# Gate b of the second half by block products, and weight sums taken one step behind their loads, in a hybrid RG-LRU/GLA decoder layer on one core

## The chip, the cores and the metric

The kernel runs on one core of a Trainium2 chip. The metric is the device time of one execution in microseconds. A profiled execution lists every instruction of the engines: PE (TensorE), PEld (its weight loads), DVE (VectorE), ACT (ScalarE), POOL (GpSimd) and SP (SyncE, which here only issues transfers).

## The reference

One decoder layer, for 1024 prompt tokens and 8 x 4 sample tokens that share the weights. All in float32, with a model width of 1024:

```python
h = rmsnorm(x, norm1_g) * (1 + sc1) + sh1
u_x, u_g, u_q, u_k, u_v, u_r, u_lr, u_ga, u_gb = split(h @ w_in)
y_a = rg_lru(causal_conv(u_x)) * gelu(u_g)          # first branch, recurrent, 1280 wide
y_b = norm(gated_linear_attention(u_q, u_k, u_v, u_lr)) * silu(u_r)   # second branch
m = sigmoid(u_ga) * (y_a @ proj_a) + sigmoid(u_gb) * (y_b @ proj_b)
x = x + gt1 * (m @ w_out)
f1, f2 = split(h2 @ ffn_w1)        # h2: x normed and modulated again, 2 x 2816 wide
x = x + gt2 * ((silu(f1) * f2) @ ffn_w2)
```

The change concerns the line with `m`: gate a (`u_ga`) with the product of the first, recurrent branch, and gate b (`u_gb`) with the product of the second.

## The kernel before, in words

Tokens lie along the free dimension. Half A has the first 512 of them, half B the other 512 and the 32 sample tokens (544, handled as two column parts of 272). Half A runs through all stages, then half B. A weight tile is 128 columns of the output: 8 chunks of 128 inputs each, 512 KB. Each is loaded as float32 into a tile of tag "raw" (five buffers, by SP), and split into a high and a low part ("hl", three buffers): the high part by ACT (L154), the low one by DVE (L155). A product then takes three passes a chunk: high by high, high by low, low by high (L452, L453, L454; L1434 to L1436 in the block products). The split has a raised priority (`AHEAD`), so that the scheduler pulls it ahead of other work on ACT and DVE.

*Products by blocks.* Some products are done for pairs of weight tiles by a Strassen-Winograd scheme: `products` makes 7 products of 4 chunks (12 matmuls each, 84 in all) where the plain way needs 8 (96). It needs sums of the inputs (`block_sums`: d0, d1, ta, tb, t12, t3, t4), and sums of weight blocks. These are made on the chip: a job loads two raw tiles, DVE makes four additions, and POOL stores the results to DRAM (`wsum` for FFN 1, `wsumg` for gates, `wsum2` for FFN 2), from where they are loaded as weights later. `weight_sums` (L348) makes them for whole tiles ("s1", "s2", four additions of 128x512, L352 to L355): 16 jobs, loads by SP in the "raw" buffers, sums right behind the load. `paced_sums` (L362) does half tiles of 256 or 384 columns in buffers of their own (tag "sums", two): a copy on POOL (L387) of one element of a tile just made, `pace[0]`, holds a job's loads (L388) until there; then the sums (L392 to L396) and the stores (L398); each job is taken in two steps, load and sum.

*The stages.* `branches` of a half runs the recurrent and attention branches; then `merge_b`: for each of eight tiles j the gate b (`gbps`, tanh), and the second branch's product (`pbps`, weights `proj_b`), both multiplied into `mb`, with the recurrent chain (`lru`: ug, ux, g tiles) filled in between. Then half A does `merge_a`: for each j gate a (`gaps`), the product of the recurrent branch (`paps`, two weight tiles pa0 and pa1 of 5 chunks), `join` (L1264, L1265: multiply by the gate, add to mb), `keep_m` (split of the sum). Half B does `merge_a_fast`: the first four recurrent products are held in SBUF (`pa`), and gate a is done by blocks (`gates_fast`, four blocks: `ha`, `hb`, `hc` in PSUM, `gc`, `gd` in SBUF), with the other four recurrent products behind the last blocks. Then `back`: `out_proj` (wops), norm, FFN.

Who does what when: PE's order in the block products is as written (`as_written`); elsewhere a scheduler orders each engine's work by priority and by modelled times, and buffers are taken as they come free. Each engine and each transfer queue then works strictly in its order. `behind(last)` pins an instruction behind work that was traced before it.

## Time and profile before

| what | value |
|---|---|
| three runs | 1957.03, 1960.13, 1961.34 us; median 1960.13 |
| profiled execution | 1958.39 us; its span 1956.6 us, mean granted clock 0.997 |
| busy in the span | PE 98%, PEld 90%, DVE 70%, ACT 50%, POOL 7% |
| half A's gate stage (`merge_a`) | 452.4 to 559.3 us |
| half B's `merge_b` with the recurrent chain | 1272 to 1424 us |
| half B's four held products, then gate a by blocks | 1424 to 1454, 1454 to 1527.5 us |
| full sum jobs on DVE | 16, from 272.2 to 771.7 us |

A row of the timeline reads: start in us, duration, engine, line, operation, output<-inputs, shapes; in brackets the idle time of the engine just before it and what ended it. Matmuls are pipelined, so the durations of neighbours overlap, and the distance between two starts is the pace.

### The profile page before, as it was taken

What the parts mean: (1) busy time and instruction counts of PE and PEld (TensorE: products, weight loads), DVE (VectorE), ACT (ScalarE), POOL (GpSimd) and SP (SyncE); (2) the same over time, 40 slices, a digit from 0 to 9 for tenths busy, and PEclk for the clock granted to TensorE, in tenths of its full rate; (3) what the DMA queues carried; (4) which work ended last, traced back from release to release, by engine and by line L of the source; (5) the groups of instructions that cost most, each with busy time, mean ns of one, the idle gap of its engine ahead of it and who ended that gap; (6) DMA issues with size and microseconds to landing.
All of it is one profiled execution on the core that took longest, in us unless ns stands there. A gap on an engine that the chain in (4) does not pass through costs nothing. (4 is left out here: it accounts for less than half of the span.)

```text
span 1956.6 us, 33960 instructions
## 1 busy us (share of the span) xinstructions
PE 1923.5 (98%) x13380; PEld 1754.8 (90%) x13380; DVE 1360.1 (70%) x2420; ACT 972.6 (50%) x1559; POOL 144.6 (7%) x279
## 2 busy tenths in 40 slices
PE   8999999998999999999999999999999999999997
PEld 5877777787899998998899998999999999999997
DVE  5648587765658774677664497786467688888867
ACT  4536376552235552555353366675245354656653
POOL 0000002111200000000000101031201000000000
PEclk9999999999999999999999999999999999999999
DMA  8344326567864467554331413334447534555553
GB/s 342 116 154 172 117 90 245 176 211 240 292 201 157 129 184 243 193 183 149 119 123 65 146 50 101 124 114 153 140 143 226 198 130 133 176 171 179 177 163 104
DMA packets 122240, 319.24 MB, mean 163 GB/s; under 512 B 14560, under 2 KB 29664, under 8 KB 122080
## 3 DMA queue, kind: packets, MB, share of 16 engines
q1 hardware_dynamic: 107536, 263.89, 41.6%
q0 software_dynamic: 14000, 52.62, 7.5%
q8 instruction: 105, 1.72, 0.4%
q10 hardware_dynamic: 544, 0.56, 0.1%
q14 instruction: 55, 0.45, 0.1%
HBM read 278.42 MB, written 38.59 MB: 162 GB/s over the span
## 5 line engine op out<-in xcount | busy, mean ns | idle before, releaser
L155 DVE TENSOR_TENSOR fwa_hl<-fwa,fwa_hl 128x1024 fp32r<-128x1024 f32 (+1 forms) x57 | 68.8, 1207 | 44.6 <-ACT fwa_hl L154 41.2
L155 DVE TENSOR_TENSOR fwb_hl<-fwb,fwb_hl 128x1024 fp32r<-128x1024 f32 (+1 forms) x64 | 77.2, 1207 | 27.7 <-ACT fwb_hl L154 27.4
L154 ACT ACTIVATE fwa_hl<-fwa 128x1024 fp32r<-128x1024 f32 (+1 forms) x57 | 59.3, 1040 | 44.0 <-PE fapsa L1436 10.8
L154 ACT ACTIVATE fwb_hl<-fwb 128x1024 fp32r<-128x1024 f32 (+1 forms) x64 | 66.6, 1041 | 23.4 <-PE fcpsb L1436 9.0
L452 PE MATMUL f3psa<-faa,f3a_hl 128*128 128x512 f32 x176 | 68.6, 390 | 0.6 <-ACT f3a_hl L154 0.6
L454 PE MATMUL f3psa<-faa,f3a_hl 128*128 128x512 f32 x176 | 68.5, 390 | 0.4 <-DVE f3a_hl L155 0.4
L453 PE MATMUL f3psa<-faa,f3a_hl 128*128 128x512 f32 x176 | 68.6, 390 | 0.0
L154 ACT ACTIVATE f3a_hl<-f3a_raw 128x768 fp32r<-128x768 f32 (+1 forms) x32 | 25.3, 792 | 55.7 <-PE f3psa L454 47.3
L155 DVE TENSOR_TENSOR f3a_hl<-f3a_raw,f3a_hl 128x768 fp32r<-128x768 f32 (+1 forms) x32 | 28.3, 888 | 17.0 <-ACT f3a_hl L154 16.7
L452 PEld LDWEIGHTS f3psa<-faa,f3a_hl 128*128 128x128 f32 x176 | 33.0, 188 | 7.8 <-ACT f3a_hl L154 1.0
L454 PEld LDWEIGHTS f3psa<-faa,f3a_hl 128*128 128x128 f32 x176 | 33.0, 188 | 7.6 <-DVE f3a_hl L155 0.9
L453 PEld LDWEIGHTS f3psa<-faa,f3a_hl 128*128 128x128 f32 x176 | 33.0, 188 | 6.8
L352 DVE TENSOR_TENSOR s_raw<-s_raw 128x512 f32<-128x512 f32 x16 | 11.1, 691 | 40.2 <-DMA s_raw<-in_ffn 40.2
L454 PE MATMUL wopsb<-mb,wob_hl 128*128 128x272 f32 x128 | 36.9, 288 | 0.0
L452 PE MATMUL wopsb<-mb,wob_hl 128*128 128x272 f32 x128 | 36.9, 289 | 0.0
L453 PE MATMUL wopsb<-mb,wob_hl 128*128 128x272 f32 x128 | 36.8, 288 | 0.0
L453 PE MATMUL wopsa<-ma,woa_hl 128*128 128x256 f32 x128 | 36.4, 284 | 0.0
L454 PE MATMUL wopsa<-ma,woa_hl 128*128 128x256 f32 x128 | 36.2, 283 | 0.0
L452 PE MATMUL wopsa<-ma,woa_hl 128*128 128x256 f32 x128 | 36.1, 283 | 0.0
L1621 POOL DMA_DIRECT2D out_yb<-yb x4 | 2.9, 720 | 407.5 <-DVE yb L1618 406.8
L452 PE MATMUL uxpsa<-h1a,uxpsa_hl 128*128 128x512 f32 x80 | 32.3, 403 | 0.0
L155 DVE TENSOR_TENSOR fvb_hl<-fvb,fvb_hl 128x768 fp32r<-128x768 f32 x28 | 26.8, 956 | 7.7 <-ACT fvb_hl L154 7.4
(2404 smaller groups left out, 7975.3 us busy)
## 6 DMA issues: line engine op xcount, KB each, us to landing
ada<-in_ada_w SPq DMA_DIRECT2D x48, 512.0 KB, 5.5
fwb<-wsum SPq DMA_DIRECT2D x72, 256.0 KB, 3.6
s_raw<-in_ffn SPq DMA_DIRECT2D x32, 512.0 KB, 4.1
wsum<-s_raw POOLq DMA_DIRECT2D x32, 512.0 KB, 3.9
fwa<-wsum SPq DMA_DIRECT2D x64, 256.0 KB, 3.3
fwb<-in_ffn SPq DMA_DIRECT2D x54, 256.0 KB, 3.6
fwa<-in_ffn SPq DMA_DIRECT2D x48, 256.0 KB, 3.2
woa_raw<-in_w_out SPq DMA_DIRECT2D x13, 512.0 KB, 3.5
```

Source lines behind the costliest of these rows:

```text
L154: act.activation(hl[:, 0, :n], raw[:, :n], AF.Copy)
L155: dve.tensor_sub(hl[:, 1, :n], raw[:, :n], hl[:, 0, :n].bitcast(F32))
L352: dve.tensor_add(r2[:, 512:1024], r2[:, 0:512], r2[:, 512:1024])
L452: pe.matmul(out, wh, x[:, o:o + w], start=st, stop=False)
L453: pe.matmul(out, wh, x[:, N + o:N + o + w], start=False, stop=False)
L454: pe.matmul(out, wl, x[:, o:o + w], start=False, stop=en)
L1621: (queues[j // 2 % len(queues)]).dma_start(out[:, j:j + 2, o:o + w], y2)
```

## The change

- Half B's `merge_b` is replaced by `branch_b`, which makes only the second branch's products and copies them to mb by ACT. Then the four held recurrent products, then `merge_fast`: gate b by four blocks (`k`), multiplied into mb, then gate a by four blocks (`h`) as before. Half B's recurrent chain is moved ahead by three steps before `branch_b`.
- Weight sums for gate b are needed too: 28 half jobs instead of 20. Five (before: four) begin in half A's `merge_b`, seven (four) in its `merge_a`, four (none) beside half A's `ffn1_fast`, eight (eight) in `branch_b`, four (four) in the gate b blocks.
- All jobs go through `Jobs`: a step makes the sums of the job before, then begins the next one's loads. The loads of a full job are issued by POOL instead of SP. Half A's `merge_a` begins full jobs at j = 0 to 4 instead of 0, 1, 3, 4, 6.
- The input rows of gate b's weights are put into the same order as gate a's (`KORD`).
- The first step of `block_sums` is made ahead of the first held product.

```diff
@@ -345,17 +345,39 @@
 
         return t[:, :HP].rearrange("p (m u n) -> p m u n", u=2, n=P)[:, :, u, :]
 
-    def weight_sums():
-
-        for f in range(FAST[0], NF):
-            r1, r2 = load_raw(I["ffn1"][2 * f], 1024, f"s1{f}"), load_raw(I["ffn1"][2 * f + 1], 1024, f"s2{f}")
-            dve.tensor_add(r2[:, 512:1024], r2[:, 0:512], r2[:, 512:1024])
-            dve.tensor_sub(r2[:, 0:512], r1[:, 0:512], r2[:, 0:512])
-            dve.tensor_sub(r1[:, 0:512], r2[:, 512:1024], r1[:, 0:512])
-            dve.tensor_sub(r1[:, 512:1024], r1[:, 512:1024], r1[:, 0:512])
-            pool.dma_start(wsum[f][:, 0:1024], r1)
-            pool.dma_start(wsum[f][:, 1024:2048], r2)
-            yield 1
+    class Jobs:
+
+        def __init__(s, jobs):
+            s.jobs, s.sums = iter(jobs), None
+
+        def finish(s):
+            if s.sums:
+                s.sums()
+            s.sums = None
+
+        def step(s):
+            s.finish()
+            job = next(s.jobs, None)
+            if job:
+                s.sums = job()
+
+    def full_sums(f):
+        def begin():
+            r1, r2 = [wp.tile([P, 1024], F32, tag="raw", name=f"s{k}{f}_raw", bufs=5) for k in "12"]
+            for r, t in (r1, 2 * f), (r2, 2 * f + 1):
+                pool.dma_start(r, I["ffn1"][t])
+
+            def sums():
+                last = len(traced())
+                dve.tensor_add(r2[:, 512:1024], r2[:, 0:512], r2[:, 512:1024])
+                behind(last)
+                dve.tensor_sub(r2[:, 0:512], r1[:, 0:512], r2[:, 0:512])
+                dve.tensor_sub(r1[:, 0:512], r2[:, 512:1024], r1[:, 0:512])
+                dve.tensor_sub(r1[:, 512:1024], r1[:, 512:1024], r1[:, 0:512])
+                pool.dma_start(wsum[f][:, 0:1024], r1)
+                pool.dma_start(wsum[f][:, 1024:2048], r2)
+            return sums
+        return begin
 
     pace = [None]
 
@@ -377,28 +399,35 @@
         for f in range(FAST[1], FAST[0]):
             columns(wsum[f], [I["ffn1"][2 * f + v] for v in range(2)])
         rows(0)
-        for c in range(GATES):
-            columns(wsumg[c], [I["w_in"][T_GA + 2 * c + v] for v in range(2)])
+        for t in (T_GB, T_GA):
+            for c in range(GATES):
+                columns(wsumg[t, c], [I["w_in"][t + 2 * c + v] for v in range(2)])
         rows(1)
-        for k, (u, src, to) in enumerate(jobs):
+        return [half_sums(k, *job) for k, job in enumerate(jobs)]
+
+    def half_sums(k, u, src, to):
+        def begin():
             r = [wp.tile([P, 768], F32, tag="sums", name=f"sums{k}{v}", bufs=2) for v in range(2)]
             rv = [t[:, :2 * u].rearrange("p (n u) -> p n u", n=2) for t in r]
             for v in range(2):
-                pool.tensor_copy(r[v][:, 0:1], pace[0][:, 0:1])
+                if pace[0] is not None:
+                    pool.tensor_copy(r[v][:, 0:1], pace[0][:, 0:1])
                 pool.dma_start(rv[v], src[v])
-            yield 1
-            r1, r2 = rv
-            last = len(traced())
-            dve.tensor_add(r2[:, 1], r2[:, 0], r2[:, 1])
-            behind(last)
-            dve.tensor_sub(r2[:, 0], r1[:, 0], r2[:, 0])
-            dve.tensor_sub(r1[:, 0], r2[:, 1], r1[:, 0])
-            dve.tensor_sub(r1[:, 1], r1[:, 1], r1[:, 0])
-            for v in range(2):
-                pool.dma_start(to[v], rv[v])
-            yield 1
-
-    sums_of, sums_late = weight_sums(), paced_sums()
+
+            def sums():
+                r1, r2 = rv
+                last = len(traced())
+                dve.tensor_add(r2[:, 1], r2[:, 0], r2[:, 1])
+                behind(last)
+                dve.tensor_sub(r2[:, 0], r1[:, 0], r2[:, 0])
+                dve.tensor_sub(r1[:, 0], r2[:, 1], r1[:, 0])
+                dve.tensor_sub(r1[:, 1], r1[:, 1], r1[:, 0])
+                for v in range(2):
+                    pool.dma_start(to[v], rv[v])
+            return sums
+        return begin
+
+    sums_of, sums_late = Jobs([full_sums(f) for f in range(FAST[0], NF)]), Jobs(paced_sums())
 
     class Half:
         def __init__(s, hf):
...
@@ -1191,17 +1220,15 @@
                 for t, p in s.over(tg, ps):
                     act.activation(t, p, AF.Tanh, scale=0.5)
 
-            lag = 1 - s.hf
-            if lag:
-                first(0)
+            first(0)
             for j in range(KD):
                 n = f"{s.n}{j}"
-                if j + lag < KD:
-                    first(j + lag)
-                if s.hf or 3 <= j < 7:
+                if j + 1 < KD:
+                    first(j + 1)
+                if j >= 3:
                     pace[0] = tgs[j]
-                    next(sums_late, None)
-                if j + lag < KD:
+                    sums_late.step()
+                if j + 1 < KD:
                     yield 5.2
                 tg = tgs.pop(j)
                 p2 = s.wide("pbps" + n)
@@ -1210,10 +1237,23 @@
                 for (t, p), (o, _) in zip(s.over(tg, p2), s.over(m, p2)):
                     dve.scalar_tensor_tensor(o, t, 1.0, p, op0=OP.add, op1=OP.mult)
                 s.mb.append(m)
-                if s.hf or 3 <= j < 7:
-                    next(sums_late, None)
-                if s.hf == 0 and j < 7:
-                    next(sums_of, None)
+                sums_of.step() if j < 7 else sums_of.finish()
+                yield 5.2
+
+        def branch_b(s):
+
+            s.mb = []
+            pace[0] = None
+            for j in range(KD):
+                n = f"{s.n}{j}"
+                sums_late.step()
+                ps = s.wide("pbps" + n)
+                s.gemm(ps, load_w(I["proj_b"][j], 1024, "pb" + n), 8, s.y_b)
+                m = xp.tile([P, 544], F32, tag="X", name="mb" + n)
+                for o, p in s.over(m, ps):
+                    act.activation(o, p, AF.Copy)
+                s.mb.append(m)
+                pace[0] = m
                 yield 5.2
 
         def gate_a(s, j):
...
@@ -1274,37 +1314,40 @@
             s.m = []
             for j in range(KD):
                 tg = s.gate_a(j)
-                if 1 <= j < 5:
-                    next(sums_late, None)
+                sums_late.step() if j < 7 else sums_late.finish()
                 s.join(j, tg, s.over(tg, s.branch_a(j)))
                 s.keep_m(j)
-                if 1 <= j < 5:
-                    next(sums_late, None)
-                if j % 3 < 2 and j < 7:
-                    next(sums_of, None)
-
-        def merge_a_fast(s):
+                if j < 6:
+                    sums_of.step() if j < 5 else sums_of.finish()
+
+        def merge_fast(s):
 
             s.m = []
             N, b, held = s.N, s.block_sums(s.h, "h"), []
...
+                next(b, None)
                 t = two[:, j * N:(j + 1) * N] if j < 2 else T(f"pa{s.n}{j}")[:, :N]
                 for o, p in s.over(t, s.branch_a(j)):
                     act.activation(o, p, AF.Copy)
                 held.append(t)
-                next(b, None)
             drain(b)
             units = []
-            for c in range(GATES):
-                w1, w2, sm = I["w_in"][T_GA + 2 * c], I["w_in"][T_GA + 2 * c + 1], wsumg[c]
-                units += [w1[:, 0:512], sm[:, 1536:2048], sm[:, 0:512], sm[:, 512:1024], sm[:, 1024:1536], w1[:, 512:1024],
-                          w2[:, 512:1024]]
+            for g in (T_GB, T_GA):
+                for c in range(GATES):
+                    w1, w2, sm = I["w_in"][g + 2 * c], I["w_in"][g + 2 * c + 1], wsumg[g, c]
+                    units += [w1[:, 0:512], sm[:, 1536:2048], sm[:, 0:512], sm[:, 512:1024], sm[:, 1024:1536], w1[:, 512:1024],
+                              w2[:, 512:1024]]
             begin = len(traced())
             product = s.products(units, 512, s.bs, "gw" + s.n)
             for c in range(GATES):
-                tgs = s.gates_fast(c, product)
-                next(sums_late, None)
+                tgs = s.gates_fast("k", c, product)
+                sums_late.step()
+                for m, t in zip(s.mb[2 * c:], tgs):
+                    dve.scalar_tensor_tensor(m[:, :N], t[:, :N], 1.0, m[:, :N], op0=OP.add, op1=OP.mult)
+            sums_late.finish()
+            for c in range(GATES):
+                tgs = s.gates_fast("h", c, product)
                 if c == GATES - 1:
                     s.keep_m(*range(2 * c))
                 for i in range(2):
@@ -1312,9 +1355,6 @@
                     s.join(j, tg, [(tg[:, :N], held[j])] if j < 4 else s.over(tg, s.branch_a(j)))
                     if c == GATES - 1:
                         s.keep_m(j)
-                    if j >= 4:
-                        next(sums_late, None)
-            drain(sums_late)
...
@@ -1557,6 +1597,9 @@
                     s.late = tg
                 else:
                     s.keep(f, tg)
+                if s.hf == 0 and f in (13, 15, 17, 19):
+                    pace[0] = tg
+                    sums_late.step()
                 yield 4.5
             as_written(begin, (mybir.EngineType.PE,))
 
@@ -1643,7 +1686,8 @@
                 drain(s.ffn1_fast(range(FAST[0], 11)))
                 for j, _ in enumerate(s.ffn2(0, 11, s.whole)):
                     if j % 2 == 0:
-                        next(sums_of, None)
+                        sums_of.step()
+                sums_of.finish()
                 return
...
@@ -1672,7 +1716,10 @@
-            for w in s.merge_b():
+            if s.hf:
+                for _ in range(3):
+                    next(l, None)
+            for w in s.branch_b() if s.hf else s.merge_b():
                 next(l, None)
                 next(l, None)
                 s.ada(1)
...
```

What stands where on the engines' queues now, at three places. First, DVE in half A's `merge_a` around the split of gate tile 3 (gapsa3_hl; papsa2 is the recurrent product of tile 2, which PE does just before gate tile 3; s1.. and s2.. are a full job's raw tiles, sums.. a half job's). Before:

```order
L352 TENSOR_TENSOR s215_raw_4111<-s215_raw_4111 128x512
L396 TENSOR_TENSOR sums40_3861<-sums40_3861 128x384
L353 TENSOR_TENSOR s215_raw_4111<-s115_raw_4109,s215_raw_4111 128x512
L155 TENSOR_TENSOR gapsa3_hl_4022<-gapsa3_raw_4020,gapsa3_hl_4022 128x1024
L354 TENSOR_TENSOR s115_raw_4109<-s215_raw_4111,s115_raw_4109 128x512
L355 TENSOR_TENSOR s115_raw_4109<-s115_raw_4109 128x512
L155 TENSOR_TENSOR pa0a3_hl_4060<-pa0a3_raw_4058,pa0a3_hl_4060 128x640
L1264 SCALAR_TENSOR_TENSOR gaa2_3959<-gaa2_3959,papsa2_3967 128x512
```

Now:

```order
L424 TENSOR_TENSOR sums60_3883<-sums60_3883 128x384
L1304 SCALAR_TENSOR_TENSOR gaa2_3975<-gaa2_3975,papsa2_3989 128x512
L1305 TENSOR_TENSOR mba2_2934<-gaa2_3975,mba2_2934 128x512
L155 TENSOR_TENSOR gapsa3_hl_4048<-gapsa3_raw_4046,gapsa3_hl_4048 128x1024
L189 TENSOR_TENSOR ma2_4032<-mba2_2934,ma2_4032 128x512
L372 TENSOR_TENSOR s214_raw_3942<-s214_raw_3942 128x512
L420 TENSOR_TENSOR sums71_3984<-sums71_3984 128x384
L374 TENSOR_TENSOR s214_raw_3942<-s114_raw_3941,s214_raw_3942 128x512
L422 TENSOR_TENSOR sums71_3984<-sums70_3983,sums71_3984 128x384
```

The split of gate tile 3 stood ahead of the join of tile 2 (L1264), and stands right behind it (L1304, L1305) now; the same holds for gate tiles 4 and 5. The full job's sums stand behind the split now, and are those of an earlier load.

Second, DVE in half B's gate blocks where a half job's sums stand among the splits of the weights (gwb.., one for 24 matmuls). Before, in the second of the four blocks (gcb1, gdb1):

```order
L1246 TENSOR_TENSOR gdb1_14525<-gdb1_14525 128x272
L392 TENSOR_TENSOR sums161_14512<-sums161_14512 128x384
L394 TENSOR_TENSOR sums161_14512<-sums160_14511,sums161_14512 128x384
L155 TENSOR_TENSOR gwb16_hl_14688<-gwb16_14685,gwb16_hl_14688 128x1024
L1245 TENSOR_TENSOR gcb1_14524<-gcb1_14524,hcpsb1_14523 128x272
L395 TENSOR_TENSOR sums160_14511<-sums161_14512,sums160_14511 128x384
L396 TENSOR_TENSOR sums160_14511<-sums160_14511 128x384
```

Now, at the end of the fourth gate b block (kcb3, kdb3) with job 26:

```order
L1286 TENSOR_TENSOR kdb3_14425<-kdb3_14425 128x272
L420 TENSOR_TENSOR sums261_14414<-sums261_14414 128x384
L422 TENSOR_TENSOR sums261_14414<-sums260_14413,sums261_14414 128x384
L155 TENSOR_TENSOR gwb30_hl_14598<-gwb30_14595,gwb30_hl_14598 128x1024
L1285 TENSOR_TENSOR kcb3_14424<-kcb3_14424,kcpsb3_14423 128x272
L423 TENSOR_TENSOR sums260_14413<-sums261_14414,sums260_14413 128x384
L1347 SCALAR_TENSOR_TENSOR mbb7_13640<-kdb3_14425,mbb7_13640 128x544
L424 TENSOR_TENSOR sums260_14413<-sums260_14413 128x384
L155 TENSOR_TENSOR gwb32_hl_14629<-gwb32_14626,gwb32_hl_14629 128x1024
```

The pattern within a block is the same: two sums, a split, the other two. It stands in five blocks one after the other now (jobs 23 to 27, the last in the first gate a block); before, only job 16 stood among the four blocks like this, and jobs 17 to 19 between the last recurrent products.

Third, POOL in half A's `merge_a`. Before, it issued the stores of a full job there, and SP its loads; now, around the stores of job 13:

```order
L414 COPY sums61_3884<-gaa1_3875 128x1
L415 DMA sums61_3884<-in_ffn2 128x768
L368 DMA s115_raw_4041<-in_ffn1 128x1024
L378 DMA wsum13_87<-s213_raw_3842 128x1024
L426 DMA wsumf20_108<-sums61_3884 128x768
L377 DMA wsum13_87<-s113_raw_3841 128x1024
L426 DMA wsumf20_108<-sums60_3883 128x768
L414 COPY sums70_3983<-gaa2_3975 128x1
L368 DMA s215_raw_4042<-in_ffn1 128x1024
```

POOL now issues the full jobs' loads (L368) too; those of job 15 stand before and behind the stores of job 13 (L378, L377).

## The prediction

> **What bounds the kernel now.** I read the page's head first, then the view of waits for PE (who ended its idle time, total, times, longest), then windows of the stages that the change touches, then single rows of PE, DVE, ACT and POOL there.

> ```profile
> span 1956.6 us, 33960 instructions
> PE 1923.5 (98%) x13380; PEld 1754.8 (90%) x13380; DVE 1360.1 (70%) x2420; ACT 972.6 (50%) x1559; POOL 144.6 (7%) x279
> ```

> ```profile
> engine line waited for: us in total, times, longest us
> PE gapsa L454 <- DVE gapsa_hl L155: 5.6, 2, 4.9
> PE hbpsb L1434 <- ACT t12hb L1408: 0.9, 1, 0.9
> PE hbpsb L1435 <- DVE t12hb L1409: 0.4, 1, 0.4
> ```

> ```profile
> core 0: us, PE busy (x), PEclk, DMA share, GB/s
> 452.00:466.00 14.00, 13.28 (x59) 1.00 0.78 269
> 466.00:471.00 5.00, 0.23 (x2) 0.91 0.11 44
> 471.00:477.00 6.00, 5.90 (x14) 0.51 0.89 309
> ...
> core 0: us, PE busy (x) PEld busy (x) DVE busy (x) ACT busy (x) POOL busy (x), PEclk, DMA share, GB/s
> ...
> 1272.00:1424.00 152.00, 152.00 (x1196) 150.57 (x1195) 101.61 (x184) 74.18 (x124) 41.49 (x71) 1.00 0.43 137
> ...
> 1454.00:1527.50 73.50, 72.27 (x577) 71.84 (x576) 51.17 (x78) 36.35 (x62) 9.52 (x22) 1.00 0.67 216
> ```

> PE is the bound: 1923.5 of 1956.6 us. So the time falls by what matmuls are taken away, and changes by what PE stands idle. In half B's stages (from 1272 us) PE is full. The one large hole is in half A's last gate stage, 466 to 471 us, and behind it PE runs at a granted clock of 0.51 for some 6 us.

> **The change part by part. 1, fewer matmuls.** Half B's eight tiles of gate b cost 48 matmuls each (8 chunks, 3 passes, 2 column parts): 384. By blocks they are 4 blocks of 7 products of 12: 336. Taken away: 48. The price of one is not its duration but its distance to the next:

> ```profile
> 1376.23 0.29 PE L452 MATMUL gbpsb4l<-h1b,gbpsb_hl 128*128 128x272 f32 x1
> 1382.21 0.29 PE L452 MATMUL pbpsb4l<-ybb,pbb_hl 128*128 128x272 f32 x1
> 1388.18 0.29 PE L452 MATMUL gbpsb5l<-h1b,gbpsb_hl 128*128 128x272 f32 x1
> ```

> A tile of 48 starts 5.98 and 5.97 us after the one before, so 0.1245 us a matmul. The blocks run at the same pace; the first snapshot of block 0 and that of block 1 on ACT:

> ```profile
> 1457.40 0.38 ACT L1442 ACTIVATE gcb<-hapsb 128x272 f32<-128x272 f32 x1
> 1467.86 0.40 ACT L1442 ACTIVATE gcb<-hapsb 128x272 f32<-128x272 f32 x1 [1.03 <-PE hapsb L1436]
> ```

> That is 10.46 us for 84, again 0.1245. Saving: 48 x 0.1245 = **-6.0 us**. The operand sums t12, on which PE waited 0.9 + 0.4 us, now begin a step earlier, beside the four held recurrent products (first DVE rows of block_sums ahead of the first of those): **-1.3**.

> **2, half A's gate stage.** The hole's origin stands on DVE: the sums of a full job (L352 to L355) wait for their load, and the split of the next gate tile (L155) stands behind them in DVE's order.

> ```profile
> 465.85 0.39 PE L453 MATMUL gapsa<-h1a,gapsa_hl 128*128 128x512 f32 x1
> 471.10 0.79 PE L454 MATMUL gapsa<-h1a,gapsa_hl 128*128 128x512 f32 x1 [4.86 <-DVE gapsa_hl L155]
> 473.40 0.63 PE L453 MATMUL gapsa<-h1a,gapsa_hl 128*128 128x512 f32 x1
> 473.82 0.63 PE L454 MATMUL gapsa<-h1a,gapsa_hl 128*128 128x512 f32 x1
> 477.55 0.39 PE L452 MATMUL gapsa<-h1a,gapsa_hl 128*128 128x512 f32 x1
> 477.77 0.39 PE L453 MATMUL gapsa<-h1a,gapsa_hl 128*128 128x512 f32 x1
> ```

> ```profile
> 451.08 0.69 DVE L352 TENSOR_TENSOR s_raw<-s_raw 128x512 f32<-128x512 f32 x1 [5.50 <-DMA s_raw<-in_ffn]
> ...
> 467.77 0.69 DVE L352 TENSOR_TENSOR s_raw<-s_raw 128x512 f32<-128x512 f32 x1 [7.95 <-DMA s_raw<-in_ffn]
> ...
> 469.83 1.22 DVE L155 TENSOR_TENSOR gapsa_hl<-gapsa_raw,gapsa_hl 128x1024 fp32r<-128x1024 f32 x1
> ...
> 472.30 0.68 DVE L1264 SCALAR_TENSOR_TENSOR gaa<-gaa,papsa 128x512 f32<-128x512 f32 x1
> ...
> 473.63 0.68 DVE L1265 TENSOR_TENSOR mba<-gaa,mba 128x512 f32<-128x512 f32 x1
> ```

> From 465.85 to 471.10 lie 5.25 us where 0.23 is the pace (477.55 to 477.77): 5.0 lost. Of the 6 us from 471 the 14 matmuls would have filled 14 x 0.227 = 3.2: 2.8 lost to the clock (pace 0.42 at 473.4). With the 0.7 of the other wait (5.6 - 4.9): 8.5 us. With sums a step behind their loads (two steps for some, by POOL's order), I expect no wait of DVE for a load there: 8.5 goes.

> But a new wait takes its place. The changed order puts the splits of gate tiles 3, 4 and 5 right behind join 2, 3 and 4 on DVE, and a join waits for the last matmul of the recurrent product that PE does just before that gate tile. Before, each split stood ahead of that join. PE then has two matmuls (0.45) that need no low part, while DVE does the join's two operations (0.68 each, L1264 and L1265 above) and the split (1.22): 2.6 less 0.45, rounded up for the handing over: 2.2 us, three times 6.6. The first wait of 0.7 stays, since the sums of job 11 now stand ahead of gate tile 0's split. Behind a gate's split stand eight sums, seven of them (four of 0.69, three of at most 0.55) ahead of the recurrent weight's split, with it some 5.5 us against the 24 matmuls' 5.4: about 0.3 in all is lost. Together 7.6 against 8.5: **-0.9**. Bounds: -7.8 (only the first 0.7 stays: a split that in fact comes early enough) and +4 (a late load on top of the joins, as long as the hole was before). I take the walk along the order, since each step in it has a row.

> **3, half B's gate phase.** Eight blocks follow each other with nothing between until the last four recurrent products. Four half jobs of 384 columns are put into the first four blocks, each summed a block later, and DVE meets these sums ahead of a weight split. One job's round: sums, store, landing, load, landing.

> ```profile
> 1474.66 0.55 DVE L392 TENSOR_TENSOR sums<-sums 128x384 f32<-128x384 f32 x1
> 1475.25 0.56 DVE L394 TENSOR_TENSOR sums<-sums,sums 128x384 f32<-128x384 f32 x1
> 1475.72 1.22 DVE L155 TENSOR_TENSOR gwb_hl<-gwb,gwb_hl 128x1024 fp32r<-128x1024 f32 x1
> ```

> ```profile
> 1390.34 0.71 POOL L398 DMA_DIRECT2D wsumg<-sums  x1 [5.21 <-DVE sums L394]
> ...
> 1395.31 0.19 POOL L387 COPY sums<-gbb 128x1 f32<-128x1 f32 x1 [0.68 <-DMA wsumg<-sums]
> 1395.54 1.43 POOL L388 DMA_DIRECT2D sums<-in_w_in  x2
> 1401.86 0.71 POOL L398 DMA_DIRECT2D wsumg<-sums  x1 [4.88 <-DVE sums L394]
> ```

> ```profile
> s_raw<-in_ffn SPq DMA_DIRECT2D x32, 512.0 KB, 4.1
> ...
> sums<-in_ffn POOLq DMA_DIRECT2D x16, 384.0 KB, 4.9
> wsumf<-sums POOLq DMA_DIRECT2D x16, 384.0 KB, 2.9
> ```

> Store to store of 256-column jobs is 11.5 us (1390.34 to 1401.86). For 384: four sums and what stands between them 3.8 to 4.6, store 2.9, copy and first issue 0.9, landing 4.9: 12.5 to 13.3, longer than the 10.46 of a block. From the phase's start, DVE reaches job 24's sums at 18.4 (a block, five products of 1.49, an add), its load being there; the rounds then put job 25's at 31.0, job 26's at 43.5, job 27's at 56.8. Job 25 costs only DVE, which is two splits ahead. For job 26 two sums and the split end at 45.8, where weight pair 15 is due at 15 x 2.99 (24 matmuls) + 0.25 = 45.1: 0.8 lost. For job 27 three sums, two adds and the split end at 60.0, against 19 x 2.99 + 0.8 + 0.25 = 57.9: 2.1 lost. With 2.9 I take **+3**. Bounds: 0 (with rounds of 11.5 job 27 is ready 4 us sooner) and +10 (each load 2.4 us later, over three rounds).

> [...]

> **4, half B's second branch.** Its eight tiles (5.97 each) now need one split (1.22) and one 256-column sum job (four of 0.42) on DVE per tile, with the recurrent chain beside them; DVE was busy 101.6 of 152 us. In exchange 8 splits and 8 merging operations leave. The copies to mb go to ACT, 74.2 busy. Only the first tile lacks a gate tile ahead of it under which its split was done: **+0.6**, bounds 0 and 3.

> **5, at nothing:** the four half jobs beside half A's FFN (4 x 4 x 0.42 on DVE, which is 70% busy over the span, and 4 MB of DMA); the other four added jobs stand in half A's two gate stages, counted above; reordered input rows (same sizes); 8 added multiplications on mb within the block, 0.72 each, where ACT and DVE are busy 36 and 51 of 73.5 us; the POOL queue, whose loads replace SP's: POOL is 7% busy.

> Sum: -6.0 - 1.3 - 0.9 + 3.0 + 0.6 = **-4.6**. The profiled execution took 1958.4 us (its span and 1.8 around it): 1953.8. It lies 1.7 below the median of the three runs (1960.1): **1955.5**. A change under 0.2% (3.9 us) can't be told from none, so "faster" is below 1956.2 and "slower" above 1964.1.

> **The rivals.** *Both stalls hidden:* half A keeps only 0.7, the half jobs are in time: -6.0 - 1.3 - 7.8 + 0.6 = -14.5, 1945.6. For it: the hole's cause (5.50 and 7.95 of waiting for a load) is really taken away, and a DVE split needs only 1.22. Against: the order of the joins.

> *Slower, by the half jobs' rounds in the gate phase.* If loads land later than 4.9 (the phase already shows a DMA share of 0.67, and weights by the SP queue share the engines), each microsecond comes back up to three times, since every job waits for the store of the one before. At 3.4 us later 3.0 + 3 x 3.4 = 13.2 us are lost, and one idle stretch passes the 4.9 us that cost 2.8 in clock: -6.0 - 1.3 - 0.9 + 0.6 + 16.0 = +8.4, 1968.5. It decides from some 11.5 us of idle PE in the eight blocks. For it: DVE really stands behind these loads; against: before, no such load was late in this stretch.

> [...]

> *Counted by durations:* if a matmul's 0.288 were its price, 13.8 are saved and 1947.7 results; the rows of the pace speak against it.

> *No measurable change:* joins and a late load cost half A 4 more than before (-6.0 - 1.3 + 4 + 3 + 0.6 = +0.3), or the gate phase 8 (+0.4): 1960.5.

> **How the numbers follow.** My forecast 0.50, with a range of its own of 1951 to 1961, of which just over half is below 1956.2; both stalls hidden 0.20; durations 0.03; no measurable change 0.09; slower by the rounds 0.18. Faster: 0.27 + 0.20 + 0.03 = 0.50; same: 0.23 + 0.09 = 0.32; slower 0.18. The range reaches to the first rival and most of the second: 1945 to 1967.

> **What would show it.** PE matmuls down by 48, and PE's busy time by about 6 us with clock 1.00. In the waits, gapsa behind DVE three times at some 2 us, none near 5, and no DVE wait of 5 us for s_raw in 450 to 560 us; a window there without a clock of 0.5. In the blocks, PE waits behind gwb_hl at the end of the b blocks and the first a block, with DVE held by sums. The prediction fails if the joins' waits aren't there, or if the sums in the blocks hold PE for over 8 us.

## The result: 4.5% slower, and the profile after

The changed kernel takes 2046.0 us (median of five runs, 2040.7 to 2052.4), beside 1959.5 for the kernel before on the same chip (1956.6 to 1961.3): a ratio of 1.0447, 95% interval 1.0416 to 1.0477. The forecast was 1955.5, in a range of 1945 to 1967. It was wrong by 90 us. The head of the profile after:

```profile
span 2044.3 us, 34088 instructions
PE 1952.3 (96%) x13332; PEld 1765.6 (86%) x13332; DVE 1383.5 (68%) x2462; ACT 992.0 (49%) x1593; POOL 192.5 (9%) x357
```

The matmuls fell by 48, as counted, and yet PE is busy 29 us longer, since part of its work ran at half clock (mean granted clock 0.981 instead of 0.997), and it is idle 92 us instead of 33. The view of waits for PE (who ended its idle time; total, times, longest) has new names at its top:

```profile
engine line waited for: us in total, times, longest us
PE gapsa L481 <- ACT gapsa_hl L154: 19.7, 5, 10.3
PE hapsb L1474 <- ACT hcb L1482: 8.9, 2, 6.7
PE gbpsa L481 <- ACT gbpsa_hl L154: 7.3, 2, 4.4
...
PE pbpsb0l L481 <- ACT trb L1127: 4.0, 1, 4.0
...
PE gapsa L483 <- DVE gapsa_hl L155: 1.1, 2, 0.5
```

The last row is the wait that the forecast priced at 6.6 us. The first is another: in half A, PE waits for the *high* part of gate a's weights (L481 is the pass that L452 was), on ACT and not on DVE. The table has each stage as the distance between the first matmuls of neighbouring stages. "Blocks" is the part of half B between the held products and `out_proj`: gate a before, both gates after. All later kernels are in the same table.

| us | second branch A | gate stage A | out, early FFN A | FFN A | half B to the blocks | blocks | span |
|---|---|---|---|---|---|---|---|
| before | 181.1 | 106.8 | 119.0 | 288.0 | 487.7 | 73.6 | 1956.6 |
| expected, no losses | 181.1 | 106.8 | 119.0 | 288.0 | 439.9 | 113.9 | |
| after | 204.5 | 136.3 | 120.7 | 305.0 | 449.2 | 128.6 | 2044.3 |
| e1_full_now | 181.1 | 133.2 | 120.5 | 288.0 | 450.4 | 124.7 | 1998.4 |
| e2_full_by_sp | 207.9 | 138.2 | 119.1 | 299.8 | 453.0 | 125.3 | 2043.7 |
| e3_rows_late | 203.9 | 137.5 | 118.6 | 300.8 | 450.3 | 113.9 | 2024.8 |
| e4_ffn_none | 207.5 | 137.7 | 118.6 | 304.0 | 451.4 | 128.9 | 2048.3 |
| e5_halves_as_before | 181.1 | 106.1 | 118.6 | 292.0 | 450.6 | 113.9 | 1962.3 |
| e6_before_full_behind | 218.1 | 130.0 | 118.9 | 301.1 | 489.2 | 73.7 | 2031.7 |
| e7_lru_six_ahead | 181.0 | 104.9 | 118.8 | 292.3 | 452.7 | 121.9 | 1971.6 |
| e8_full_spread | 181.1 | 97.9 | 120.7 | 300.4 | 452.3 | 113.9 | 1967.7 |
| e9_own_buffers | 181.1 | 113.3 | 133.5 | 293.4 | 448.3 | 129.4 | 2004.6 |
| e10_lru_before_yb | 181.1 | 105.9 | 119.1 | 292.4 | 451.9 | 113.9 | 1964.9 |
| e11_full_later | 181.2 | 108.9 | 118.9 | 291.3 | 451.4 | 113.9 | 1966.9 |
| e12_all | 181.5 | 106.3 | 118.8 | 288.0 | 456.0 | 114.0 | 1964.8 |
| e13_gate_halves_only | 181.1 | 114.8 | 119.8 | 302.5 | 452.0 | 126.0 | 1996.3 |
| e14_two_plain_gates | 181.1 | 105.4 | 118.9 | 287.9 | 464.5 | 103.4 | 1962.5 |
| e15_two_jobs_earlier | 181.0 | 106.8 | 118.7 | 288.0 | 453.2 | 103.4 | 1954.7 |

The second row is worked out: eight gate tiles of 5.97 leave half B's stretch, four blocks of 10.46 come to the blocks, and 1.5 is taken off there for the operand sums (forecast 1.3; e3, below, measures 113.9). Against it, after loses 23.4, 29.5, 1.7, 17.0, 9.3 and 14.7 us. Three quarters of the loss stand in half A, whose products the change leaves alone.

**Where half A's time went.** The timeline of after around the longest wait, rows of POOL, SP, ACT and PE in order of time:

```profile
495.66 0.54 POOL L368 DMA_DIRECT2D s_raw<-in_ffn  x1 [0.59 <-DVE gapsa_hl L155]
496.82 0.54 POOL L368 DMA_DIRECT2D s_raw<-in_ffn  x1
...
516.45 0.53 POOL L368 DMA_DIRECT2D s_raw<-in_ffn  x1 [3.10 <-DVE pa1a_hl L155]
...
520.87 0.53 POOL L377 DMA_DIRECT2D wsum<-s_raw  x1 [1.06 <-DVE s_raw L376]
...
524.47 0.33 SPq L145 DMA_DIRECT2D gapsa_raw<-in_w_in  x1
...
530.81 1.06 ACT L154 ACTIVATE gapsa_hl<-gapsa_raw 128x1024 fp32r<-128x1024 f32 x1 [14.51 <-DMA gapsa_raw<-in_w_in]
...
531.92 0.79 PE L481 MATMUL gapsa<-h1a,gapsa_hl 128*128 128x512 f32 x1 [10.25 <-ACT gapsa_hl L154]
...
535.71 0.54 POOL L378 DMA_DIRECT2D wsum<-s_raw  x1 [8.71 <-DVE s_raw L374]
...
538.57 0.54 POOL L377 DMA_DIRECT2D wsum<-s_raw  x1 [1.78 <-DVE s_raw L376]
```

Read it backwards. PE waits 10.25 us for ACT, ACT 14.51 for a weight load, and that load is issued only at 524.47. The same from SP's side (waits of its queue, 511 to 545 us):

```profile
SPq L145 <- DMA wsum<-s_raw: 12.7, 1, 12.7
```

The load waited for a *store* of a weight sum (issued at 520.87, landed some 3.6 later), because that store's source was the "raw" buffer it needed. The pair of raw tiles loaded at 495.66 and 496.82 is not stored before 535.71 and 538.57: two of the five buffers are held for 43 us. With the next pair's first tile (516.45) and the pair whose last store is the one of 520.87, the full jobs hold all five, and the gate's own weights none. Before, a job's first load and last store in this stage stood 12 us apart, on SP and POOL:

```profile
459.60 0.88 SPq L145 DMA_DIRECT2D s_raw<-in_ffn  x2
...
471.94 0.55 POOL L356 DMA_DIRECT2D wsum<-s_raw  x1 [1.91 <-DVE s_raw L355]
```

Over all 16 jobs, this distance was 24.6 to 66.8 us after (median 40) and 8.4 to 35.1 before (median 13).

Windows of after over the gate stage, the hole and what follows it show the second half of the price, the clock:

```profile
core 0: us, PE busy (x), PEclk, DMA share, GB/s
475.30:611.00 135.70, 110.30 (x431) 0.89 0.74 254
521.00:532.00 11.00, 0.75 (x4) 0.64 0.78 291
532.00:538.00 6.00, 5.96 (x14) 0.51 0.38 134
```

431 matmuls at the pace of 0.227 take 97.9 us; of the 38 us above that, 25.4 are idle and the rest half clock.

**Where the blocks' time went.** After, DVE, ACT and PE at the seam from the gate b blocks to the gate a blocks:

```profile
1535.99 0.56 DVE L420 TENSOR_TENSOR sums<-sums 128x384 f32<-128x384 f32 x1 [8.09 <-DMA sums<-in_ffn]
1536.58 0.56 DVE L422 TENSOR_TENSOR sums<-sums,sums 128x384 f32<-128x384 f32 x1
1537.06 1.22 DVE L155 TENSOR_TENSOR gwb_hl<-gwb,gwb_hl 128x1024 fp32r<-128x1024 f32 x1
1538.19 0.43 DVE L1285 TENSOR_TENSOR kcb<-kcb,kcpsb 128x272 f32<-128x272 f32 x1
...
1538.66 0.66 ACT L1287 ACTIVATE kcb<-kcb 128x544 f32<-128x544 f32 x1 [7.24 <-DVE kcb L1285]
1539.22 0.38 ACT L1482 ACTIVATE hcb<-hapsb 128x272 f32<-128x272 f32 x1
...
1539.65 0.59 PE L1474 MATMUL hapsb<-t12hb,gwb_hl 128*128 128x272 f32 x1 [6.67 <-ACT hcb L1482]
```

DVE does stand 8.09 us behind a half job's load, and PE waits, but on another path than the one I priced. Behind the sums stands the add that ends a gate b block (L1285); ACT's tanh (L1287) needs that add; behind the tanh in ACT's order stands the *next* block's snapshot (L1482), which frees the PSUM that PE needs. A job's round, sums to sums, was 13.8, 16.0 and 15.6 us (1506.17, 1519.98, 1535.99, 1551.54) where I had 12.5 to 13.3, and the loads landed later: the eight in this stretch took 5.5 to 7.7. The medians of all 16 (DMA issues: count, KB each, median us to landing) were 4.9 and 2.9 before, and are now:

```profile
sums<-in_ffn POOLq DMA_DIRECT2D x16, 384.0 KB, 6.1
wsumf<-sums POOLq DMA_DIRECT2D x16, 384.0 KB, 3.3
```

### The profile page after: what moved, and what is told of

It reads as the page before. It is cut to its first block, busy times and chain, and to the rows that moved or that the text cites. A ratio compares the mean times of both kernels' runs of the same rounds, so it can differ in the third digit from the quotient of the medians.

```text
span 2044.3 us, 34088 instructions
## 1 busy us (share of the span) xinstructions
PE 1952.3 (96%) x13332; PEld 1765.6 (86%) x13332; DVE 1383.5 (68%) x2462; ACT 992.0 (49%) x1593; POOL 192.5 (9%) x357
## 5 line engine op out<-in xcount | busy, mean ns | idle before, releaser
L155 DVE TENSOR_TENSOR fwa_hl<-fwa,fwa_hl 128x1024 fp32r<-128x1024 f32 (+1 forms) x57 | 68.8, 1206 | 42.6 <-ACT fwa_hl L154 42.0
L155 DVE TENSOR_TENSOR fwb_hl<-fwb,fwb_hl 128x1024 fp32r<-128x1024 f32 (+1 forms) x64 | 77.2, 1206 | 27.7 <-ACT fwb_hl L154 27.4
L154 ACT ACTIVATE fwb_hl<-fwb 128x1024 fp32r<-128x1024 f32 (+1 forms) x64 | 66.6, 1040 | 23.4 <-PE fcpsb L1476 9.0
L481 PE MATMUL f3psa<-faa,f3a_hl 128*128 128x512 f32 x176 | 69.2, 393 | 3.2 <-ACT f3a_hl L154 3.1
L155 DVE TENSOR_TENSOR f3a_hl<-f3a_raw,f3a_hl 128x768 fp32r<-128x768 f32 (+1 forms) x32 | 28.5, 890 | 38.1 <-ACT f3a_hl L154 38.1
L481 PE MATMUL gapsa<-h1a,gapsa_hl 128*128 128x512 f32 x64 | 29.1, 455 | 19.7 <-ACT gapsa_hl L154 19.7
L420 DVE TENSOR_TENSOR sums<-sums 128x256 f32<-128x256 f32 (+1 forms) x28 | 12.8, 459 | 45.5 <-DMA sums<-in_ffn 26.0
L481 PEld LDWEIGHTS f3psa<-faa,f3a_hl 128*128 128x128 f32 x176 | 33.1, 188 | 11.9 <-ACT f3a_hl L154 5.5
L483 PEld LDWEIGHTS f3psa<-faa,f3a_hl 128*128 128x128 f32 x176 | 33.0, 188 | 10.7 <-DVE f3a_hl L155 4.1
L155 DVE TENSOR_TENSOR gwb_hl<-gwb,gwb_hl 128x1024 fp32r<-128x1024 f32 x28 | 34.1, 1221 | 12.1 <-ACT gwb_hl L154 11.9
L368 POOL DMA_DIRECT2D s_raw<-in_ffn x32 | 17.4, 544 | 230.2 <-DVE fwa_hl L155 164.7
L481 PE MATMUL wopsb<-mb,wob_hl 128*128 128x272 f32 x128 | 36.9, 290 | 0.0
L482 PE MATMUL wopsa<-ma,woa_hl 128*128 128x256 f32 x128 | 36.4, 284 | 0.0
L483 PE MATMUL wopsa<-ma,woa_hl 128*128 128x256 f32 x128 | 36.2, 283 | 0.0
## 6 DMA issues: line engine op xcount, KB each, us to landing
ada<-in_ada_w SPq DMA_DIRECT2D x48, 512.0 KB, 5.5
s_raw<-in_ffn POOLq DMA_DIRECT2D x32, 512.0 KB, 3.9
wsum<-s_raw POOLq DMA_DIRECT2D x32, 512.0 KB, 3.5
```

The source lines that it names most:

```text
L154: act.activation(hl[:, 0, :n], raw[:, :n], AF.Copy)
L155: dve.tensor_sub(hl[:, 1, :n], raw[:, :n], hl[:, 0, :n].bitcast(F32))
L368: pool.dma_start(r, I["ffn1"][t])
L420: dve.tensor_add(r2[:, 1], r2[:, 0], r2[:, 1])
L481: pe.matmul(out, wh, x[:, o:o + w], start=st, stop=False)
L482: pe.matmul(out, wh, x[:, N + o:N + o + w], start=False, stop=False)
```

## The experiments

The first four take one part of the change away each. **e1_full_now**: full jobs by SP and summed at once, at before's places; all else as changed.

```diff
-            r1, r2 = [wp.tile([P, 1024], F32, tag="raw", ...) for k in "12"]
-            for r, t in (r1, 2 * f), (r2, 2 * f + 1):
-                pool.dma_start(r, I["ffn1"][t])
+            r1, r2 = load_raw(I["ffn1"][2 * f], 1024, f"s1{f}"), load_raw(...)
...
+    class Now(Jobs):
+        def step(s):
+            job = next(s.jobs, None)
+            if job:
+                job()()
...
-                if j < 6:
-                    sums_of.step() if j < 5 else sums_of.finish()
+                if j % 3 < 2 and j < 7:
+                    sums_of.step()
```

> The changed kernel with the full jobs as before: loads by SP, sums right behind them, begun at j = 0, 1, 3, 4, 6 of half A's gate stage; all else as changed. Theory 1 (full jobs one step behind hold up to four of the five raw buffers, and weight loads wait until the sums' stores have landed): half A's second-branch stage goes from 204.5 back to some 181 us, its gate stage from 136.3 to some 108 with the old hole of 5 us, FFN A a little down; 2046 to about 1995. Rival 2 (the added half jobs on POOL and in the transfers make half A slow): both stages stay above 195 and 125, time above 2025. Rival 3 (the splits behind the joins, as predicted): it was never more than 7 us, so above 2035.

2000.5 us, 1.0209 of before [1.0188, 1.0229]. The second-branch stage and the FFN are back at 181.1 and 288.0 to the tenth: their 40 us were the full jobs'. The four half jobs beside the FFN are still there, so they cost nothing. The gate stage stays at 133.2, with waits (for PE, then for DVE from 452 to 586 us) that are no longer those for ACT:

```profile
PE papsa L486 <- DVE pa1a_hl L155: 12.8, 5, 4.4
PE gapsa L486 <- DVE gapsa_hl L155: 11.1, 4, 4.2
```

```profile
DVE sums L416 <- DMA sums<-in_ffn: 21.7, 3, 9.7
DVE sums L416 <- DMA sums<-in_w_in: 18.6, 3, 7.2
DVE s_raw L369 <- DMA s_raw<-in_ffn: 13.2, 4, 6.2
```

DVE, in its order, stands behind half jobs *and* full jobs, 53.5 us in these rows. Some 108 was expected: a second cause lies under the first in this stage.

**e2_full_by_sp**: the full jobs' loads on SP's queue again, still summed a step later.

```diff
-                pool.dma_start(r, I["ffn1"][t])
+                sp.dma_start(r, I["ffn1"][t])
```

> The changed kernel with one edit: the full jobs' loads are issued by SP instead of POOL; sums stay one step behind. Theory 1 (raw buffers held): little is won, within 15 us of 2046, SP still waits for the landing of the stores. Rival (POOL's queue order, where a load stands behind copies and stores, makes the loads late): half A's two stages come back to some 181 and 110 us, about 2000.

2045.0 us, 1.043 [1.0400, 1.0461]: nothing gained. The queue is not the cause; the step between load and sums is.

**e3_rows_late**: the last four half jobs among the gate a blocks and the last recurrent products, as before (`half_steps` loads a job, and sums it a step later).

```diff
                 tgs = s.gates_fast("k", c, product)
-                sums_late.step()
+                sums_late.finish()
...
+            sl = half_steps(sums_late)
             for c in range(GATES):
                 tgs = s.gates_fast("h", c, product)
+                next(sl, None)
...
+                    if j >= 4:
+                        next(sl, None)
```

> The changed kernel with one edit: the last four half jobs (384 columns) are taken out of the gate b blocks and put where they were before, among the gate a blocks and the last four recurrent products. Theory (DVE waits for these loads ahead of the add that the tanh and the next block's first snapshot wait for): the phase of the eight blocks goes from 128.6 us to 115.4 to 118, 11 to 13 us less in all: about 2034. Rival (the eight blocks in a row lack DVE or weight-load time anyway): the phase stays above 125.

2028.6 us, 1.0354 [1.0329, 1.0379]. The blocks take 113.9. Their 912 matmuls at 0.1245 are 113.5, so that nothing much is lost: the 14.7 us there were these four jobs' place.

**e4_ffn_none**: no half jobs beside half A's FFN. The sums of these four jobs are not made; other blocks' sums are read in their place.

```diff
-                if s.hf == 0 and f in (13, 15, 17, 19):
-                    pace[0] = tg
-                    sums_late.step()
```

> The changed kernel without the four half jobs beside half A's FFN; the third and fourth gate b block of half B use the weight sums of the first and second instead (four jobs less in all, same reads). Theory (these jobs take the two sums buffers that the FFN's held products use, and the full jobs' loads stand on POOL behind them): half A's FFN goes from 305 to 288 to 293 us, about 2032. Rival (the 17 us come from the full jobs one step behind, which go on in this stage): FFN stays above 300, time above 2040.

2044.3 us, 1.0428 [1.0397, 1.0459]; FFN 304.0 beside 305.0. So "at nothing" holds for these four.

**e6_before_full_behind**: the other direction, the kernel before with only the full jobs one step behind their loads, by POOL, begun at the change's places.

```diff
-    sums_of, sums_late = weight_sums(), paced_sums()
+    sums_of, sums_late = Jobs([full_sums(f) for f in range(FAST[0], NF)]), paced_sums()
...
-                if j % 3 < 2 and j < 7:
-                    next(sums_of, None)
+                if j < 6:
+                    sums_of.step() if j < 5 else sums_of.finish()
```

> The kernel before with one part of the change alone: full jobs one step behind their loads, loads by POOL. Theory (raw buffers): the second-branch stage of half A goes from 181 to some 204 us, FFN A from 288 to 300 to 305, the gate stage from 107 to 110 to 125, 1960 to about 2000 to 2015. Rival (these losses need the change's added half jobs): within 1955 to 1970.

2038.3 us, 1.0403 [1.0387, 1.0420]. This part alone makes the span 75 us longer (40 to 55 were expected): 37.0, 23.2 and 13.1 in the three stages with full jobs.

**e9_own_buffers**: the changed kernel, with the full jobs in two buffers of their own and three for the rest.

```diff
-            r1, r2 = [wp.tile(..., tag="raw", name=f"s{k}{f}_raw", bufs=5) ...]
+            r1, r2 = [wp.tile(..., tag="fs", name=f"s{k}{f}_raw", bufs=2) ...]
...
-        raw = wp.tile([P, 1024], F32, tag="raw", name=name + "_raw", bufs=5)
+        raw = wp.tile([P, 1024], F32, tag="raw", name=name + "_raw", bufs=3)
...
```

> The changed kernel with one edit: the full jobs have two buffers of their own, and the raw weights three instead of five (the same memory in all); loads by POOL, sums one step behind. Theory 1 (weight loads wait for the landing of the sums' stores, because jobs and weights take turns in five buffers): half A's second-branch stage falls from 204 to 181 to 190 us, FFN A from 305 to 290; the gate stage stays above 125, since DVE stands behind the half jobs' loads there all the same; about 2000 to 2015. Rival (a step behind is slow for another reason: DVE's order, or the transfers of POOL): the second-branch stage stays above 198. If three raw buffers are too few for the weights, half B gets slower by more than 5 us.

2008.3 us, 1.0251 [1.0235, 1.0266]. Order, queue and step as changed, and yet 181.1, 113.3 and 293.4: sharing the buffers is what costs. Three are too few elsewhere (`out_proj` waits 6.2 and 3.9 us), which takes 13 back. The gate stage was expected above 125 and came to 113.3. What PE still waits there it waits for DVE (10.1 us), and DVE's own waits now have another at their top than one for loads (455 to 569 us):

```profile
DVE gaa L1304 <- POOL sums L414: 36.0, 6, 8.6
```

The join (L1304) overwrites the gate tile of which the pace copy (L414) reads one element, and that copy waits on POOL until stores of sums have landed. So the copy that holds a job's loads back holds DVE too: 36.0 us here, and in after, beside the waits for weights, 7.1.

**e13_gate_halves_only**: e1 without any full job in the gate stage (eight beside the second branch, two and six beside the FFN), to see the half jobs alone at their new places.

```diff
-                if j % 3 < 2 and j < 7:
-                    sums_of.step()
...
+                if s.hf == 0 and f in (8, 10):
+                    sums_of.step()
...
-                    if j % 2 == 0:
+                    if j < 6:
                         sums_of.step()
```

> As the first run (full jobs at once, by SP: 2000.5), but with no full job in half A's gate stage (eight in the second-branch stage, two beside FFN 1, six beside FFN 2); the seven half jobs of that stage stay. Theory A (half and full jobs hold each other up: a half job's loads stand on POOL behind a full job's stores, which wait for DVE, which stands behind another half job's sums): the gate stage falls from 133 to 105 to 115 us. Theory B (the row of half jobs alone, whose round is longer than a step's 12.25): it stays at 120 to 133. FFN A costs some 8 to 12 more, as it did when two full jobs stood beside FFN 1.

1998.8 us, 1.0204 [1.0184, 1.0223]. The gate stage takes 114.8, still 17 above its clean 97.9; DVE waits there for the half jobs' loads (452 to 567 us):

```profile
DVE sums L416 <- DMA sums<-in_ffn: 30.9, 4, 9.3
DVE sums L416 <- DMA sums<-in_w_in: 25.6, 4, 7.6
```

Sums to sums took 12.7 and 14.6 us (464.98, 477.67, 492.30), a tile of this stage 12.25: one step behind is not enough where, as here, a step is shorter than a round. That is read from these rows; a second pair of buffers for the half jobs, which would let a round begin earlier, was not tried. Alone these jobs cost 17, with full jobs summed at once between them (e1) 35. There POOL's order links the two, as e1's rows suggest: a half job's loads stand behind a full job's store, which waits for DVE.

```profile
473.27 0.54 POOL L374 DMA_DIRECT2D wsum<-s_raw  x1 [8.38 <-DVE s_raw L370]
473.81 1.67 POOL L410 COPY sums<-gaa 128x1 f32<-128x1 f32 x2
475.43 1.08 POOL L411 DMA_DIRECT2D sums<-in_ffn  x2
```

**e5_halves_as_before**: e1 and e3 together, half jobs in half A at before's places, and eight beside the FFN. Of the change it keeps gate b by blocks.

```diff
-                sums_late.step() if j < 7 else sums_late.finish()
+                if 1 <= j < 5:
+                    sums_late.step()
                 s.join(j, tg, s.over(tg, s.branch_a(j)))
                 s.keep_m(j)
+                if 1 <= j < 5:
+                    sums_late.finish()
...
-                if s.hf == 0 and f in (13, 15, 17, 19):
+                if s.hf == 0 and f in (7, 9, 11, 13, 15, 17, 19, 21):
```

> The changed kernel with the full jobs as before, the last four half jobs late (both as in the two runs above), and half A's half jobs at the places of the kernel before: four in the second-branch stage, four in the gate stage, loads and sums within one step; the eight that are left stand beside half A's FFN. Theory (the gate stage lost 26 us to a row of half jobs, one in every step, whose round of 13 to 16 us is longer than a step's 12.25 and behind whose loads DVE stands): the gate stage falls from 133 to some 107 us, the second-branch stage stays at 181, FFN at 288 to 290, the eight blocks at 114; the time falls to that of before, 1958 to 1963. Rival (the gate stage's splits behind the joins, or the split order at large, cost it): the stage stays above 120, time above 1970. Rival (the FFN can't hide eight jobs): FFN above 295.

1963.4 us, 1.0020 [1.0002, 1.0037]. Half A's gate stage is back at 106.1. The 6.0 + 1.5 us are still not seen: four come back in the FFN (eight half jobs there, not four), and 10.7 in half B (450.6 beside 439.9). The next six runs look for these.

**e7_lru_six_ahead** and **e10_lru_before_yb**: e5, with half B's recurrent chain six steps ahead of the second branch instead of three; or three, but ahead of the splits of y_b.

```diff
-                for _ in range(3):
+                for _ in range(6):
```

```diff
-            s.y_b_tiles()
             if s.hf:
                 for _ in range(3):
                     next(l, None)
+            s.y_b_tiles()
```

> As the run with the half jobs as before, but half B's recurrent chain six steps ahead of the second branch instead of three. Theory (PE's 4.0 us at the first second-branch tile is a wait for the PSUM that an activation of the recurrent chain reads, which stands behind the eight splits of y_b; with no gate tile to fill it the clock falls too): with the chain further ahead the stretch from half A's end to the blocks falls from 450 to 440 to 445 us, 5 to 10 us faster than that run. Rival (the stretch lacks work for PE wherever the chain stands): within 3 us of that run.

> As the run with the half jobs as before (1963.4), with one edit: in half B the three steps of the recurrent chain stand ahead of the eight splits of y_b, not behind them. Theory (ACT reads the PSUM that the first second-branch tile needs only behind DVE's and ACT's eight splits of y_b, 10 us of work): PE's wait of 3.9 us there and the slow clock behind it go, the stretch from half A's end to the blocks falls from 450.6 to 441 to 445 us, 1955 to 1958. Rival (now the first tile waits for y_b as long): within 2 us of that run.

1973.1 us, 1.0074 [1.0059, 1.0090], and 1966.1, 1.0023 [1.0009, 1.0037]. In after and e5, PE waits 4 us at the first second-branch product, for PSUM that ACT empties late, since y_b's eight splits stand ahead on ACT and DVE (after):

```profile
1352.95 4.47 ACT L188 ACTIVATE ybb<-srb 128x544 fp32r<-128x544 f32 x8
...
1361.54 0.49 ACT L1127 ACTIVATE trb<-g1b6l,vh 128x272 f32<-128x272 f32 x1 [2.61 <-DVE lab L1158]
```

With the chain ahead of the splits PE waits for the splits themselves (e10):

```profile
PE pbpsb0l L491 <- ACT ybb L188: 5.1, 1, 5.1
```

Moving the chain only renames the wait (in e7 PE waits 5.5 us at g1b7l). While y_b is split PE needs work that doesn't depend on it, and that had been the gate b tile that the change takes away. In e7 a gate b block waits as well (kapsb behind DVE, 5.4 us).

**e8_full_spread**, **e11_full_later**: e5, with the gate stage's full jobs at j = 3 and 6 (two more beside FFN 1, the rest beside FFN 2), or at 2, 3, 4, 6.

```diff
-                if j % 3 < 2 and j < 7:
+                if j in (3, 6):
...
+                if s.hf == 0 and f in (8, 10):
+                    sums_of.step()
```

```diff
-                if j % 3 < 2 and j < 7:
+                if j in (2, 3, 4, 6):
```

> As the run with the half jobs as before, but the full jobs are taken out of half A's gate stage as far as possible: eight in the second-branch stage, two in the gate stage (j = 3 and 6), two beside FFN 1 (f = 8 and 10), four beside FFN 2. Theory (the old hole of 5 us and its 3 us of half clock come from DVE standing behind a full job's load at j = 1): the gate stage falls from 107 to some 99 us, 6 to 8 us faster than that run. Rival (the wait moves with the job): the gate stage or FFN loses as much elsewhere, no difference.

> As the run with the half jobs as before (1963.4), with one edit: the full jobs of half A's gate stage at j = 2, 3, 4 and 6 (before 0, 1, 3, 4, 6), and one more in the second-branch stage; FFN untouched. Theory (only the job begun at j = 0, behind the last ones of the stage before, makes the old hole): gate stage 106 to 98 to 101 us, 1956 to 1958. Rival (the hole moves to another j): gate stage above 104.

1968.1 us, 1.0049 [1.0034, 1.0064], and 1965.4, 1.0033 [1.0020, 1.0046]. e8 empties the gate stage wholly (97.9, 8.2 better than e5) and pays 8.4 beside the FFN. e11 moves the hole (gapsa behind DVE, longest 6.5). Both had been expected to gain 5 us or more.

**e12_all**: e10 and e11, and the four extra FFN jobs beside half B's r tiles.

```diff
-                if s.hf == 0 and f in (7, 9, 11, 13, 15, 17, 19, 21):
+                if s.hf == 0 and f in (13, 15, 17, 19):
...
-            r = weave(s.r_tiles(), s.adas, 3)
+            r = weave(side(s.r_tiles(), steps_of(sums_late)) if s.hf else s.r_tiles(), s.adas, 3)
```

> The two edits above together, and four of the eight half jobs beside half A's FFN moved into half B's attention stage (beside its r tiles, without a pace). If the savings add: gate stage 98 to 101, FFN 288 to 289, the stretch of half B 441 to 447, the blocks 114: 1963.4 - 5 - 3 - 6 = 1946 to 1952, faster than the kernel before by 0.4 to 0.7%. If the stretch's stall stays or the four jobs cost PE there, 1955 to 1960, no difference.

1964.8 us, 1.0026 [1.0016, 1.0037]. The FFN is back at 288.0 (4.0 less than e5), half B's stretch is 5.4 longer: moved, not gone.

**e14_two_plain_gates**: e5, with the last two gate b tiles done plainly, ahead of y_b's splits; three gate b blocks, and two half jobs fewer, six of them beside the FFN. **e15_two_jobs_earlier**: also two half jobs more in half A's second branch and two fewer in half B's.

```diff
+            s.plain = {}
             if s.hf:
+                for j in (6, 7):
+                    ps = s.proj_h(T_GB + j, f"gbps{s.n}{j}")
...
             s.y_b_tiles()
```

```diff
-                if 3 <= j < 7:
+                if 1 <= j < 7:
                     pace[0] = tgs[j]
...
-                sums_late.step()
+                sums_late.step() if j < 6 else sums_late.finish()
```

> As the run with the half jobs as before (1963.4), but the last two gate b tiles of half B are done plainly (48 matmuls each) ahead of y_b's splits, and only three gate b blocks are left; two half jobs less, six beside FFN A. Matmuls: 12 more, +1.5 us. Theory (PE had nothing to do while y_b was split): the stretch before the blocks is 450.6 + 11.9 for the two tiles less 7 to 10 = 452.5 to 455.5, the gate phase 113.9 - 10.5 = 103.4, the time 1954 to 1958, level with the kernel before or up to 0.3% faster. Rival (the scheduler puts the wait elsewhere): 1963 to 1966.

> As the run with two plain gate tiles, but two half jobs more in half A's second-branch stage (six, from j = 1) and two less in half B's (six, j up to 5), so that the last of them is summed before the held recurrent products end. Theory (the split of the fourth held product's weights stands on DVE behind the sums of a late job): PE's wait of 4.5 us at papsb3 goes, with the clock's share the stretch falls from 464.5 to 456 to 459, 1954 to 1957, 0.1 to 0.3% faster than the kernel before. Rival (lack of DVE time, or the two jobs cost half A as much): 1961 to 1965.

e14: 1962.6 us, 1.0010 [0.9998, 1.0022]. The wait at the first second-branch product falls from 4.0 to 0.6. But the last held product, which waited 1.6 us in after and 1.7 in e5, now waits 4.5 for a split behind a half job's sums (PE, DVE):

```profile
1416.68 0.43 DVE L416 TENSOR_TENSOR sums<-sums 128x256 f32<-128x256 f32 x1 [7.28 <-issue]
...
1419.27 0.60 PE L493 MATMUL papsb3l<-yab,pa0b_hl 128*128 128x272 f32 x1 [4.49 <-DVE pa0b_hl L155]
```

e15 takes that job away, and with it the wait: half B's stretch falls from 464.5 to 453.2, 1.4 above what it would be without losses (439.9 + 2 x 5.97). It takes 1956.4 us, 0.9986 [0.9976, 0.9997], the only version below before: by 0.14%, less than the 0.2% that I count as a difference, and it is the lowest of fifteen kernels with the change or a part of it.

## Why the prediction was wrong, point by point

**1, fewer matmuls: right.** 48 fewer. Before, the stretch of the blocks had 576 matmuls, 71.7 us at 0.1245, and took 73.6; in e3 it has 912, 113.5 us, and takes 113.9. So the price of a matmul holds, and the earlier operand sums save 1.5 (1.3 forecast).

**2, half A's gate stage: the step that failed.** It is the sentence "With sums a step behind their loads ... I expect no wait of DVE for a load there: 8.5 goes". For the full jobs it is nearly true, and I took the wait away without asking what the waiting sums hold. They hold raw buffers, which every weight load of half A needs: 43 us a pair instead of 12. That is -0.9 against +29.5 in this stage (e9 gives 23.0 of it back), and what "at nothing" in part 5 missed in the second-branch stage and the FFN (+23.4, +17.0). e1, e6 and e9 show it from three sides, and e2 takes the queue out. The trace of before had the row for it: a job's load at 459.60 and its store at 471.94, with five buffers. The joins that I priced at 6.6 cost 1.1, which doesn't test that walk, since the high part came late in their place; in e9, where it came in time, gapsa waits 2.3 in two waits, and the join stands behind POOL, which the walk had not. A second failure in the same step: a half job's round (12.7 to 14.6) is longer than a step of this stage (12.25), so that "a step behind" does not take DVE's wait away. e13 shows that the half jobs cost 17 alone, and DVE's waits for their loads; that the round is the reason is argued.

**3, the gate phase: the right place, mis-sized.** 3 forecast, 14.7 measured. The rival "slower, by the half jobs' rounds" had 16.0 for this stretch, close to what came, and in part by luck, since its path was different: not the weight's split, but a chain of three engines in their order (DVE's add, ACT's tanh, ACT's snapshot, PSUM).

**4, half B's second branch: the right sign, mis-sized.** 0.6 forecast (bounds 0 to 3), 9.3 measured: I covered the first tile's *weight* split and not y_b's eight, which a plain gate tile had covered before. PE's wait there is 4.0 us, with some 2.6 of half clock behind it (granted clock 0.50 from 1360.5 to 1367.2 us); 1.6 more is the last held product's wait for its split. e14 and e15 show both, by giving gate tiles back and by taking the late job away.

**5, at nothing:** right for four half jobs beside the FFN (e1, e4), wrong for the full jobs. "POOL is 7% busy" was true, and e2 shows that the queue was not at fault.

The rivals were all about stalls that I had already seen. None was about buffers, so that none could reach 2046.

## What to carry to other kernels

Before a consumer is moved behind its load, price what it holds meanwhile: buffers x holding time (here a pair of raw buffers for 43 us instead of 12), against the other users of the same pool. With buffers for one job at a time, as here, set a step against the whole round of load, sums, store and buffer release: in e13, where rounds of 12.7 and 14.6 us met steps of 12.25, DVE, which has the sums in its order, still stood 30.9 and 25.6 us behind loads (that the round is the reason is argued, not shown). A copy that paces transfers by reading a tile also held back the engine that overwrites that tile: DVE, by 36.0 us in e9. And when products are taken away to save PE time, look for what they covered: e8 to e12 moved the same few microseconds from stage to stage, and only work given back to PE at the uncovered place (e14, e15) kept a part of the saving.
